# Two layer norms' neighbours reordered: when late weights are split, and in which order a product's three terms run

## The chip, the core and the metric

The kernel runs on one core of a Trainium2 chip. The core has a matrix engine (TensorE, PE in the profile, with its weight loads as PEld), a vector engine (VectorE, DVE), a scalar engine (ScalarE, ACT), GpSimd (POOL) and SyncE (SP), which here issues nearly all of the DMAs. Each engine works through its own queue in the order of the program, and waits on semaphores for the others. The metric is the device time of one execution in microseconds (us); lower is better.

## The reference, cut to what matters

One step of a two-layer decoder on 512 prompt rows and 8 sample rows, 1024 wide. Layer 0 mixes tokens with windowed attention, layer 1 with gated linear attention (GLA). A gated feed-forward net (FFN, 2816 wide) follows each, and a layer norm follows each mixer and each net.

```python
def layer_norm(x, g, b):
    mu = jnp.mean(xf, -1, keepdims=True)
    var = jnp.mean(jnp.square(xf - mu), -1, keepdims=True)
    return (xf - mu) * lax.rsqrt(var + LN_EPS) * g + b
...
def conv_ffn(x, buf, w_up, conv_w, conv_b, w_down):
    h = x @ w_up
    a, u = h[..., :D_FF], h[..., D_FF:]
    ap = jnp.concatenate([buf, a], axis=1)
    c = conv_b + sum(conv_w[j] * ap[:, j:j + T] for j in range(CONV_W))
    return (jax.nn.gelu(c, approximate=False) * u) @ w_down, ap[:, T:]
...
    for i in range(DEPTH):
        mix = swa(x) if i % 2 == 0 else gla_mix(x)
        x = layer_norm(ALPHA * x + mix, ln_mix_g[i], ln_mix_b[i])
        x = layer_norm(ALPHA * x + conv_ffn(x), ln_ffn_g[i], ln_ffn_b[i])
```

All of it is in float32, and the products keep nearly that precision. The kernel splits each operand into a high part in a shorter format (fp32r) and a low part, the rest, and sums three products: high by high, weight's high by rows' low, weight's low by rows' high.

## The kernel before, in words

**Tiles.** Activations lie transposed, 128 features by rows. The rows are in two groups: a (256 prompt rows; tiles `x_a`, `xs_a`) and b (256 prompt rows and the 8 sample rows; `x_b`, `xh_b`, `xl_b`). For group a high and low parts share the tile `xs_a`.

**Units.** The weights are cut into 187 units of 128 output columns. A unit is loaded by SP into one of two `raw` tiles (L160). ACT writes its high part `wh` and DVE its low part `wl = raw - wh`. The two lines for this are L165 and L168, or, for "late" units, L177 and L179 in `parts`. Units 0 to 9 are attention's, 10 to 17 its output product, 18 to 85 the first net, 86 (the small rank weight) to 110 GLA, 111 to 118 its output product, 119 to 186 the second net. Six `wts` slots hold units. At the start of each net one more unit (24 and 125) goes into an extra slot.

**Loop.** `order` (L970 onwards) interleaves the groups: group a runs ahead of group b by four or five units. At the start of the first net the steps are a18 to a23, b18, a24, b19, a25 and so on, where a18 is group a's product with unit 18. After each step of group b a further unit is loaded.

**Product.** `product` makes 24 matmuls of a unit, for eight slices of 128 features: L193 (high by high), L195 (rows' low), L196 (weight's low). For group a and the first unit of a net the rows' low parts come after all others, at L198. From the fifth pair of a net on, group a uses `product2` (L214, L215).

**Norm.** `ln_chunk` adds the output product and sums up; `ln_end` ends the norm. PE means the sums (L283), ACT takes mean and square (L291, L292), DVE the negated variance `nv` (L295), ACT logarithm and exponential (L304, L305), DVE refines the root (L311, L312) into `rp` (L314). Then for each of eight slices DVE scales (`x_b`, L333), ACT writes the high part (`xh_b`, L334) and DVE the low part (`xl_b`, L335). The first product of group b in the next phase needs `xh_b`. POOL subtracts the mean from six of the slices (L294).

**The net's steps.** For a gate unit ACT copies PE's result (L616) and starts the convolution (L621), DVE adds two taps (L622, L623), ACT takes GELU (L632, whose function table must be loaded first). For the value unit that follows, DVE multiplies (L644), and ACT and DVE split the result (L221, L222).

**What sets the order.** Within a stretch of code a scheduler places each engine's instructions by its own estimate of when operands are ready. `issue_after(ins)` makes what is written inside it stand behind `ins` in the same engine's queue. `parts` uses this for the five units loaded around a norm (19 to 23, 87 to 91, 120 to 124). While `norm` holds, for `HOLD` steps after group a's norm, the high parts go behind group a's exponential. The low part of the first goes behind group a's last `x_a`, the others behind its last low row. `norm[4]` is the number of the first of these units.

Of the kernel before, what the change touches and what calls it, by code (L numbers as in the profile page):

```python
# [14 lines left out]
AF = mybir.ActivationFunctionType  # L15
# [5 lines left out]
P = 128  # L21
D = 1024
KD = 8
# [31 lines left out]

LATEB = 14

HOLD = 5

WIDE = 4  # L60

# [16 lines left out]
def parted(rows):  # L78

    return rows.rearrange("p (j t) -> p t j", t=2)  # L80


def in_turn(rows):

    return rows.rearrange("p t j -> p j t")
# [10 lines left out]
class Net:  # L96
# [74 lines left out]
    def parts(self, u, h, l, r):  # L171


        norm = self.norm if self.norm and self.slot < self.norm[0] else None
        behind = lambda ins: self.tc.issue_after(ins) if norm else ExitStack()
        with behind(norm and norm[1]):
            self.nc.scalar.activation(h, r, AF.Copy)  # L177
        with behind(norm and norm[2 if u == norm[4] else 3]):
            self.nc.vector.tensor_tensor(l, r, h.bitcast(F32), op=ALU.subtract)  # L179
        yield from ()  # L180

    def product(self, g, u, rh, rl):
        nc = self.nc
        h, l = self.w[u]
        nt = self.units[u][1]

        tail = g.i == 0 and u in self.phases[2::3]
        ps = self.acc.tile([P, 512], F32, name="accp")
        o = ps[:, :g.n].rearrange("p (j t) -> p j t", t=2)
        for k in range(nt):  # L190
            ks = slice(k * P, (k + 1) * P)
            xh, xl = in_turn(rh[:, k]), in_turn(rl[:, k])
            nc.tensor.matmul(o, h[:, ks], xh, start=k == 0, stop=False)  # L193
            if not tail:
                nc.tensor.matmul(o, h[:, ks], xl, start=False, stop=False)  # L195
            nc.tensor.matmul(o, l[:, ks], xh, start=False, stop=not tail and k == nt - 1)  # L196
        for k in range(nt) if tail else ():
            nc.tensor.matmul(o, h[:, k * P:(k + 1) * P], in_turn(rl[:, k]), start=False, stop=k == nt - 1)  # L198
        return ps[:, :g.n]

    def product2(self, g, u, rs, rh, rl, wide):
# [76 lines left out]
    def ln_end(self, g, i, last=False):  # L278
        nc, n, x = self.nc, g.n, g.x
        yield 0 if g.i and not last else 1  # L280
        e1, e2 = self.mtile("tp")[:, :n], self.mtile("pv")[:, :n]
        for e, sums, rest in ((e1, g.s1, x[:, KD - 1]), (e2, g.s2, g.q)) if last else ((e1, g.s1, None), (e2, g.s2, None)):
            nc.tensor.matmul(e, self.ones_a, sums, start=True, stop=rest is None)  # L283
            if rest is not None:
                nc.tensor.matmul(e, self.ones_a, rest, start=False, stop=True)
        t = lambda name, b=1: self.ln.tile([P, NT - 256], F32, name=name, bufs=b)[:, :n]
        mu, q, nv, r = t("mu"), t("msq"), t("nv"), t("r")
        if last:

            nv, vr = self.mtile("sc")[:, :n], self.mtile("sc")[:, :n]  # L290
        nc.scalar.copy(mu, e1)  # L291
        nc.scalar.activation(q, e1, AF.Square)  # L292
        for m in range(2, NSUB) if last else range(NSUB):
            nc.gpsimd.tensor_tensor(x[:, m], x[:, m], mu, op=ALU.subtract)  # L294
        nvi = nc.vector.scalar_tensor_tensor(nv, q, LN_EPS, e2, op0=ALU.subtract, op1=ALU.subtract)  # L295

        with self.tc.issue_after(nvi.ins):
            if last:
                for xp in (x[:, 0:2], x[:, NSUB:KD]):
                    nc.vector.tensor_tensor(xp, xp, e1.unsqueeze(1).broadcast_to([P, 2, n]), op=ALU.subtract)  # L300
            else:
                for m in range(NSUB, KD):
                    nc.vector.tensor_tensor(x[:, m], x[:, m], e1, op=ALU.subtract)
        nc.scalar.activation(r, nv, AF.Ln, scale=-1.0)  # L304
        self.exp = nc.scalar.activation(r, r, AF.Exp, scale=-0.5).ins  # L305
        if last:
            nc.vector.tensor_tensor(vr, nv, r, op=ALU.mult)
            q = nv
            nc.vector.scalar_tensor_tensor(q, vr, 0.5, r, op0=ALU.mult, op1=ALU.mult)
        else:  # L310
            nc.vector.tensor_tensor(q, r, r, op=ALU.mult)  # L311
            nc.vector.scalar_tensor_tensor(q, q, 0.5, nv, op0=ALU.mult, op1=ALU.mult)  # L312
        rp = e2
        nc.vector.scalar_tensor_tensor(rp, q, 1.5, r, op0=ALU.add, op1=ALU.mult)  # L314
        sc = lambda m: self.par[:, C_LNG + i * KD + m:C_LNG + i * KD + m + 1]
        bi = lambda m: self.par[:, C_LNB + i * KD + m:C_LNB + i * KD + m + 1]
        if last:

            behind = None
            for m in range(0, KD, 2):  # L320
                xp = x[:, m:m + 2]
                with self.tc.issue_after(behind) if behind else ExitStack():
                    nc.vector.tensor_tensor(xp, xp, rp.unsqueeze(1).broadcast_to([P, 2, n]), op=ALU.mult)
                for j in (m, m + 1):
                    if j in (0, 1, 2, 4, 6):
                        nc.scalar.activation(x[:, j], x[:, j], AF.Identity, scale=sc(j), bias=bi(j))
                    else:
                        behind = nc.vector.tensor_scalar(x[:, j], x[:, j], sc(j), bi(j), op0=ALU.mult, op1=ALU.add).ins
                nc.sync.dma_start(out=self.O["y"][:, m:m + 2, g.c0:g.c0 + n], in_=xp)
            return  # L330

        for m in range(KD):
            v = nc.vector.scalar_tensor_tensor(x[:, m], x[:, m], sc(m), rp, op0=ALU.mult, op1=ALU.mult)  # L333
            nc.scalar.activation(g.xh[:, m], parted(x[:, m]), AF.Identity, bias=bi(m))  # L334
            xl = nc.vector.scalar_tensor_tensor(g.xl[:, m], parted(x[:, m]), bi(m), g.xh[:, m].bitcast(F32), op0=ALU.add, op1=ALU.subtract)  # L335
        if g.i == 0:
            self.norm = self.slot + HOLD, self.exp, v.ins, xl.ins, self.next_phase() + 1
        for m in range(KD):
            yield 1 if m else LATEB
            self.tc.keep_in_program_order(nc.gpsimd.tensor_scalar(x[:, m], x[:, m], 1.0, bi(m), op0=ALU.mult, op1=ALU.add))  # L340
# [655 lines left out]
    def next_unit(self, extra):  # L996
        u = self.nu
        if u < len(self.units):
            self.nu += 1
            done = u - WSLOTS  # L1000
            late = not extra and self.units[u][1] and any(e - 5 <= done < e for e in (*self.phases[2:3], *self.phases[3:4], *self.phases[5:6]))
            self.load_unit(u, extra=extra, late=late)
            if extra:
                self.extra[u] = True
# [147 lines left out]
```

## Time and profile before

| | |
|---|---|
| median of 3 runs | 1142.89 us (1142.06 to 1144.12) |
| the profiled execution's own time | 1142.6 us |
| its span, first to last instruction | 1140.9 us |
| mean granted TensorE clock | 0.990 of full |
| DVE, ACT, POOL busy | 68%, 50%, 28% of the span |

The span is what the profile's times are counted in, from 0. The profiled execution took 1.7 us more than its span, and lies 0.3 us under the median. Three norms stand between phases: the one before the first net (about 155 to 195 us), the one before GLA (515 to 558) and the one before the second net (755 to 795). A fourth ends the program and isn't touched.

### The profile page before, as it was taken

How to read it: one execution, taken by the hardware profiler on the slowest of the kernel's cores; microseconds unless marked ns; L12 is line 12 of the kernel's file. 1: busy time of each engine (PE TensorE's matmuls, PEld its weight loads, DVE VectorE, ACT ScalarE, POOL GpSimd, SP SyncE). 2: the span in 40 equal slices, each digit the busy share in tenths (PEclk: the TensorE clock that was granted, in tenths of full speed). 3: DMA queues.
4: the chain of work that ended last, by engine and by line, in shares of the span. 5: the costliest groups of instructions: out<-in, count | busy, mean ns of one | idle time of the engine just before them, and what ended most of it. 6: DMA issues, size and time to landing. Idle time of an engine off the chain costs nothing.

```text
span 1140.9 us, 22909 instructions
## 1 busy us (share of the span) xinstructions
PE 1103.6 (97%) x8806; PEld 1055.0 (92%) x8806; DVE 779.6 (68%) x1630; ACT 566.6 (50%) x1251; POOL 316.0 (28%) x585
## 2 busy tenths in 40 slices
PE   8998998999999999999899999998999999999996
PEld 7997798999999999999899899898999999999995
DVE  8897578755665566668867777788755665466566
ACT  5677556524553245435545555456534553245433
POOL 4575584400110011354311101274400110001242
PEclk9999999999999999999899999999999999999998
DMA  7463022333233233243124355432323323223222
GB/s 244 147 182 90 15 75 94 111 95 129 93 100 105 92 104 101 75 133 96 54 88 151 114 183 161 129 109 93 112 93 117 105 93 104 100 93 112 75 64 75
DMA packets 53788, 122.81 MB, mean 108 GB/s; under 512 B 6792, under 2 KB 27312, under 8 KB 53680
## 3 DMA queue, kind: packets, MB, share of 16 engines
q1 hardware_dynamic: 51664, 119.61, 32.5%
q10 hardware_dynamic: 2016, 1.75, 0.5%
q8 instruction: 69, 1.13, 0.4%
q14 instruction: 39, 0.32, 0.1%
HBM read 108.67 MB, written 8.47 MB: 103 GB/s over the span
## 4 chain that ended last, share of the span: by engine, by line
PE 75%; DVE 11%; DMA 6%; ACT 4%; issue 2%; POOL 1%; SPq 1%; ACTq 0%; DVEq 0%; POOLq 0%
PE accp L195 15%; PE accp L214 15%; PE accp L196 15%; PE accp L193 15%; PE accp L215 8%; DMA vb<-dv 3%; DVE wl L168 1%; DVE xs_a L335 1%; DMA qs<-hl 1%; DVE wl L179 1%; DVE sgla L889 1%; DMA raw<-in_w_qkv 1%; DMA raw<-in_w_up 1%; DVE x_a L333 1%; PE pv L533 1%
## 5 line engine op out<-in xcount | busy, mean ns | idle before, releaser
L168 DVE TENSOR_TENSOR wl<-raw,wh 128x1024 fp32r<-128x1024 f32 (+2 forms) x174 | 210.4, 1211 | 109.2 <-ACT wh L165 108.5
L165 ACT ACTIVATE wh<-raw 128x1024 fp32r<-128x1024 f32 (+2 forms) x170 | 175.8, 1034 | 208.9 <-PE accp L195 187.0
L193 PE MATMUL accp<-xh_b,wh 128*128 128x264 f32 x976 | 271.7, 278 | 6.5 <-ACT xh_b L334 6.5
L195 PE MATMUL accp<-xl_b,wh 128*128 128x264 f32 x976 | 270.7, 278 | 0.2 <-DVE xl_b L335 0.2
L196 PE MATMUL accp<-xh_b,wl 128*128 128x264 f32 x976 | 270.5, 277 | 0.0
L214 PE MATMUL accp<-xs_a,wh 128*128 128x512 f32 x576 | 196.3, 382 | 0.0
L193 PEld LDWEIGHTS accp<-xh_b,wh 128*128 128x128 f32 x976 | 184.9, 189 | 7.4 <-ACT xh_b L334 6.8
L195 PEld LDWEIGHTS accp<-xl_b,wh 128*128 128x128 f32 x976 | 184.5, 189 | 2.9 <-DVE xl_b L335 0.4
L196 PEld LDWEIGHTS accp<-xh_b,wl 128*128 128x128 f32 x976 | 184.4, 189 | 0.8 <-issue 0.6
L215 PE MATMUL accp<-xs_a,wl 128*128 128x256 f32 x576 | 145.4, 273 | 0.0
L193 PE MATMUL accp<-hh_b,wh 128*128 128x264 f32 x480 | 133.9, 279 | 1.8 <-ACT hh_b L221 1.3
L195 PE MATMUL accp<-hl_b,wh 128*128 128x264 f32 x480 | 134.4, 280 | 0.3 <-DVE hl_b L573 0.2
L196 PE MATMUL accp<-hh_b,wl 128*128 128x264 f32 x480 | 133.5, 278 | 0.0
L214 PEld LDWEIGHTS accp<-xs_a,wh 128*128 128x128 f32 x576 | 109.1, 189 | 11.4
L193 PE MATMUL accp<-xs_a,wh 128*128 128x256 f32 x400 | 112.9, 284 | 2.1 <-ACT wh L165 0.9
L196 PE MATMUL accp<-xs_a,wl 128*128 128x256 f32 x400 | 111.6, 281 | 1.6 <-DVE wl L168 1.1
L215 PEld LDWEIGHTS accp<-xs_a,wl 128*128 128x128 f32 x576 | 110.2, 191 | 1.9
L195 PE MATMUL accp<-xs_a,wh 128*128 128x256 f32 x384 | 107.9, 281 | 0.0
L193 PEld LDWEIGHTS accp<-hh_b,wh 128*128 128x128 f32 x480 | 91.3, 190 | 2.5 <-ACT hh_b L221 1.7
L195 PEld LDWEIGHTS accp<-hl_b,wh 128*128 128x128 f32 x480 | 91.2, 190 | 1.8 <-DVE hl_b L573 0.4
L196 PEld LDWEIGHTS accp<-hh_b,wl 128*128 128x128 f32 x480 | 91.3, 190 | 0.2
L225 POOL COPY hist<-aext 128x2 f32<-128x2 f32 x44 | 10.8, 245 | 276.8 <-DVE aext L620 274.0
(331 smaller groups left out, 2488.8 us busy)
## 6 DMA issues: line engine op xcount, KB each, us to landing
raw<-in_w_up SPq DMA_DIRECT2D x88, 512.0 KB, 3.4
raw<-in_w_down SPq DMA_DIRECT2D x32, 512.0 KB, 3.4
raw<-in_w_gla SPq DMA_DIRECT2D x24, 512.0 KB, 3.4
raw<-in_w_mix_o SPq DMA_DIRECT2D x16, 512.0 KB, 4.0
raw<-in_w_down SPq DMA_DIRECT2D x16, 384.0 KB, 3.1
qs<-hl SPq DMA_DIRECT2D x64, 64.0 KB, 2.1
sgla<-in_state_gla SPq DMA_DIRECT2D x16, 256.0 KB, 2.8
vb<-dv SPq DMA_DIRECT2D x16, 256.0 KB, 3.8
```

What stands on the lines that cost most here:

```text
L165: nc.scalar.activation(h[:, c], r[:, c], AF.Copy)
L168: nc.vector.tensor_tensor(l[:, c], r[:, c], h[:, c].bitcast(F32), op=ALU.subtract)
L179: self.nc.vector.tensor_tensor(l, r, h.bitcast(F32), op=ALU.subtract)
L193: nc.tensor.matmul(o, h[:, ks], xh, start=k == 0, stop=False)
L195: nc.tensor.matmul(o, h[:, ks], xl, start=False, stop=False)
L196: nc.tensor.matmul(o, l[:, ks], xh, start=False, stop=not tail and k == nt - 1)
L214: both = lambda: nc.tensor.matmul(o, h[:, ks], in_turn(rs[:, k].rearrange("p t q j -> p t (q j)")), start=k == 0, stop=last)
L215: low = lambda: nc.tensor.matmul(o[:, :P], l[:, ks], in_turn(rh[:, k]), start=False, stop=False)
L333: v = nc.vector.scalar_tensor_tensor(x[:, m], x[:, m], sc(m), rp, op0=ALU.mult, op1=ALU.mult)
L335: xl = nc.vector.scalar_tensor_tensor(g.xl[:, m], parted(x[:, m]), bi(m), g.xh[:, m].bitcast(F32), op0=ALU.add, op1=ALU.subtract)
L533: mm = nc.tensor.matmul(pv[64 * v:64 * v + 64, b * P:(b + 1) * P], self.vtok[:, kb, 64 * v:64 * v + 64], parts[v][w][:, b], start=i == 0, ...
L889: late(nc.vector.scalar_tensor_tensor(s[:, j], vb[:, j], kraw[:, b:b + 1], s[:, j], op0=ALU.mult, op1=ALU.add))
```

## The change

```diff
-HOLD = 5
+HOLD = 6
+
+LOWS = 7
...
         norm = self.norm if self.norm and self.slot < self.norm[0] else None
         behind = lambda ins: self.tc.issue_after(ins) if norm else ExitStack()
-        with behind(norm and norm[1]):
+
+        n = u - norm[4] if norm else 0
+        with behind(norm and (*[norm[1]] * 4, self.square, self.exp)[n]):
             self.nc.scalar.activation(h, r, AF.Copy)
-        with behind(norm and norm[2 if u == norm[4] else 3]):
+        with behind(norm and (norm[2], *[norm[3]] * 4, self.rest)[n]):
             self.nc.vector.tensor_tensor(l, r, h.bitcast(F32), op=ALU.subtract)
...
-        tail = g.i == 0 and u in self.phases[2::3]
+        tail = u in self.phases[2::3] or g.i and u in self.phases[2:4]
+        behind = g.i == 0 and nt == KD and not tail and any(e < u < e + LOWS for e in (*self.phases[2:4], *self.phases[5:6]))
...
-            nc.tensor.matmul(o, l[:, ks], xh, start=False, stop=not tail and k == nt - 1)
-        for k in range(nt) if tail else ():
-            nc.tensor.matmul(o, h[:, k * P:(k + 1) * P], in_turn(rl[:, k]), start=False, stop=k == nt - 1)
+            if not behind:
+                nc.tensor.matmul(o, l[:, ks], xh, start=False, stop=not tail and k == nt - 1)
+        for k in range(nt) if tail or behind else ():
+            w, r = (h, rl) if tail else (l, rh)
+            nc.tensor.matmul(o, w[:, k * P:(k + 1) * P], in_turn(r[:, k]), start=False, stop=k == nt - 1)
...
-        nc.scalar.activation(q, e1, AF.Square)
+        self.square = nc.scalar.activation(q, e1, AF.Square).ins
...
+        self.rest = xl.ins
         if g.i == 0:
             self.norm = self.slot + HOLD, self.exp, v.ins, xl.ins, self.next_phase() + 1
...
-            late = not extra and self.units[u][1] and any(e - 5 <= done < e for e in (*self.phases[2:3], *self.phases[3:4], *self.phases[5:6]))
+            late = self.units[u][1] and any(e - 5 <= done < e + extra for e in (*self.phases[2:3], *self.phases[3:4], *self.phases[5:6]))
```

The parts of the late weights are tied to group b's norm as well. For the fifth (units 23, 91, 124) the high part goes behind group b's square (L292 before, L299 now). The extra unit (24, 125) becomes a sixth late one: its high part goes behind group b's exponential, its low part behind group b's last low row. GLA has no extra unit, so no sixth.

In `product`, group a's matmuls with the weight's low part come after the unit's other sixteen, for units 19 to 24, 87 to 92 and 120 to 125. Group b now takes its rows' low parts last in units 18 and 119, as group a did. No instruction is added or taken away on PE, DVE, ACT or POOL, and SP's queue keeps its order.

The change's lines have other numbers. What was L165, L168, L177, L179 is now L167, L170, L181, L183. The matmuls L193, L195, L196, L198 are L198, L200, L202, L205. From the norm on seven lines are added, from the net's steps on eight.

On ACT, in group b's norm before the first net, these rows stand one after the other before the change. `wh_2624`, `wh_2660`, `wh_2737` are the high parts of units 22, 23 and 24; `mu`, `msq`, `r` belong to the norm:

```order
L177 ACTIVATE wh_2624<-raw_2623 128x1024
L177 ACTIVATE wh_2660<-raw_2659 128x1024
L291 COPY mu_2674<-tp_2670 128x264
L292 ACTIVATE msq_2675<-tp_2670 128x264
L616 COPY aext_2832<-accp_2807 128x256
L621 ACTIVATE conv_2835<-accp_2807,par_78 128x256
L304 ACTIVATE r_2677<-nv_2676 128x264
L305 ACTIVATE r_2677<-r_2677 128x264
L632 ACT_TABLE_LOAD
L632 ACTIVATE conv_2770<-conv_2770 128x256
L165 ACTIVATE wh_2737<-raw_2736 128x1024
L632 ACTIVATE conv_2835<-conv_2835 128x256
```

And after it:

```order
L181 ACTIVATE wh_2624<-raw_2623 128x1024
L298 COPY mu_2674<-tp_2670 128x264
L299 ACTIVATE msq_2675<-tp_2670 128x264
L181 ACTIVATE wh_2660<-raw_2659 128x1024
L311 ACTIVATE r_2677<-nv_2676 128x264
L624 COPY aext_2832<-accp_2807 128x256
L629 ACTIVATE conv_2835<-accp_2807,par_78 128x256
L312 ACTIVATE r_2677<-r_2677 128x264
L640 ACT_TABLE_LOAD
L640 ACTIVATE conv_2768<-conv_2768 128x256
L181 ACTIVATE wh_2737<-raw_2736 128x1024
L228 ACTIVATE hs_a_87<-hprod_2803 128x2x128
```

The mean and the square moved ahead of unit 23's high part, and the two steps of the net that stood ahead of the logarithm now stand behind it.

On DVE, in the same norm, from `nv` to the scaled rows, before:

```order
L295 SCALAR_TENSOR_TENSOR nv<-msq,pv 128x264
L303 TENSOR_TENSOR x_b<-x_b,tp 128x264 x2
L622 SCALAR_TENSOR_TENSOR conv<-aext,par,conv 128x256
L311 TENSOR_TENSOR msq<-r 128x264
L623 SCALAR_TENSOR_TENSOR conv<-aext,par,conv 128x256
L644 TENSOR_TENSOR hprod<-conv,accp 128x256
L312 SCALAR_TENSOR_TENSOR msq<-msq,nv 128x264
L168 TENSOR_TENSOR wl<-raw,wh 128x1024
L644 TENSOR_TENSOR hprod<-conv,accp 128x256
L314 SCALAR_TENSOR_TENSOR pv<-msq,r 128x264
L222 TENSOR_TENSOR hs_a<-hprod,hs_a 128x2x128
L333 SCALAR_TENSOR_TENSOR x_b<-x_b,par,pv 128x264 x8
```

And after:

```order
L302 SCALAR_TENSOR_TENSOR nv<-msq,pv 128x264
L310 TENSOR_TENSOR x_b<-x_b,tp 128x264 x2
L183 TENSOR_TENSOR wl<-raw,wh 128x1024
L630 SCALAR_TENSOR_TENSOR conv<-aext,par,conv 128x256
L318 TENSOR_TENSOR msq<-r 128x264
L652 TENSOR_TENSOR hprod<-conv,accp 128x256
L631 SCALAR_TENSOR_TENSOR conv<-aext,par,conv 128x256
L319 SCALAR_TENSOR_TENSOR msq<-msq,nv 128x264
L229 TENSOR_TENSOR hs_a<-hprod,hs_a 128x2x128
L321 SCALAR_TENSOR_TENSOR pv<-msq,r 128x264
L652 TENSOR_TENSOR hprod<-conv,accp 128x256
L340 SCALAR_TENSOR_TENSOR x_b<-x_b,par,pv 128x264 x8
```

Unit 23's low part, which stood ahead of `nv`, comes after it. Unit 24's low part (L168) left this stretch; it stands behind the last `xl_b`.

On PE, where group b's first product (`accp_2933`) meets unit 24 of group a (`accp_2975`; `accp_2904` is unit 23), before:

```order
L195 MATMUL accp_2904<-xs_a_86,wh_2660 128x256
L196 MATMUL accp_2904<-xs_a_86,wl_2661 128x256
L193 MATMUL accp_2933<-xh_b_89,wh_2404 128x264
L193 MATMUL accp_2975<-xs_a_86,wh_2737 128x256
L195 MATMUL accp_2975<-xs_a_86,wh_2737 128x256
L196 MATMUL accp_2975<-xs_a_86,wl_2738 128x256
```

And after:

```order
L205 MATMUL accp_2904<-xs_a_86,wl_2661 128x256 x8
L198 MATMUL accp_2933<-xh_b_89,wh_2404 128x264
L202 MATMUL accp_2933<-xh_b_89,wl_2405 128x264
...
L198 MATMUL accp_2975<-xs_a_86,wh_2737 128x256
L200 MATMUL accp_2975<-xs_a_86,wh_2737 128x256
```

Before, one matmul of b18 was followed by all 24 of a24. Now two slices of b18 come first, and the other six alternate with a24's first sixteen. The first `xh_b` matmul has the same number of matmuls ahead of it as before, in all three phases.

## The prediction

> **What bounds the kernel now.** I read the page's busy shares first, then PE's list of waits, then the order of time around the three norms.
>
> ```profile
> span 1140.9 us, 22909 instructions
> PE 1103.6 (97%) x8806; PEld 1055.0 (92%) x8806; DVE 779.6 (68%) x1630; ACT 566.6 (50%) x1251; POOL 316.0 (28%) x585
> PE accp L193 <- ACT xh_b L334: 6.5, 2, 3.3
> PE accp L716 <- ACT v_a L783: 2.5, 1, 2.5
> ```
>
> PE is busy for 97% of the span. The change adds no matmul and takes none away, so it can only win idle time, 37 us in all, or clock. The list of waits (total, times, longest) says where: two waits for `xh_b`, 6.5 us together, and one of 2.5 us at GLA's start, where ACT's `v_a` copy stands behind the first `xh_b`. PE's own rows at these places, with the idle time before each in brackets:
>
> ```profile
> 188.48 0.38 PE L193 MATMUL accp<-xh_b,wh 128*128 128x264 f32 x1 [3.27 <-ACT xh_b L334]
> 191.87 0.38 PE L195 MATMUL accp<-xl_b,wh 128*128 128x264 f32 x1 [0.22 <-DVE xl_b L335]
> 787.44 0.59 PE L193 MATMUL accp<-xh_b,wh 128*128 128x264 f32 x1 [3.19 <-ACT xh_b L334]
> 784.00:787.40 3.40, 0.26 (x3) 0.07 (x1) 3.40 (x7) 1.66 (x6) 1.83 (x4) 0.99 0.28 57
> 787.40:790.60 3.20, 3.16 (x14) 3.05 (x15) 3.20 (x9) 2.98 (x7) 0.00 (x0) 0.50 0.27 109
> 556.95 0.39 PE L193 MATMUL accp<-xs_a,wh 128*128 128x256 f32 x1
> 547.50:555.90 8.40, 8.25 (x31) 6.99 (x32) 6.66 (x18) 4.26 (x11) 0.00 (x0) 0.59 0.00 0
> ```
>
> The rows with a colon are stretches of time: length, then busy time of PE, PEld, DVE, ACT and POOL, then the granted clock. After the wait at the second net the clock is 0.50 for 3.2 us. After the wait at GLA's start it is 0.59 on the mean for 8.4 us. After the equally long wait at the first net it stays at 1.00 (page and stretches show no fall there).
>
> So the question is what holds `xh_b`. ACT and DVE, first net:
>
> ```profile
> 175.62 1.06 ACT L177 ACTIVATE wh<-raw 128x1024 fp32r<-128x1024 f32 x1 [1.90 <-DMA raw<-in_w_up]
> 178.13 1.06 ACT L177 ACTIVATE wh<-raw 128x1024 fp32r<-128x1024 f32 x1 [1.45 <-DMA raw<-in_w_up]
> 179.09 0.36 ACT L291 COPY mu<-tp 128x264 f32<-128x264 f32 x1
> 180.82 0.42 ACT L304 ACTIVATE r<-nv 128x264 f32<-128x264 f32 x1 [0.34 <-DVE nv L295]
> 181.27 0.42 ACT L305 ACTIVATE r<-r 128x264 f32<-128x264 f32 x1
> 181.71 1.28 ACT L632 ACT_TABLE_LOAD   x1
> 183.01 0.42 ACT L632 ACTIVATE conv<-conv 128x256 f32<-128x256 f32 x1
> 183.33 1.06 ACT L165 ACTIVATE wh<-raw 128x1024 fp32r<-128x1024 f32 x1
> 184.59 0.46 ACT L221 ACTIVATE hs_a<-hprod 128x256 fp32r<-128x256 f32 x1
> 187.89 2.40 ACT L334 ACTIVATE xh_b<-x_b,par 128x264 fp32r<-128x264 f32 x5
> 184.69 1.76 DVE L168 TENSOR_TENSOR wl<-raw,wh 128x1024 fp32r<-128x1024 f32 x1
> 186.37 0.41 DVE L644 TENSOR_TENSOR hprod<-conv,accp 128x256 f32<-128x256 f32 x1
> 186.70 0.43 DVE L314 SCALAR_TENSOR_TENSOR pv<-msq,r 128x264 f32<-128x264 f32 x1
> 187.05 0.41 DVE L222 TENSOR_TENSOR hs_a<-hprod,hs_a 128x256 fp32r<-128x256 f32 x1
> 187.38 3.28 DVE L333 SCALAR_TENSOR_TENSOR x_b<-x_b,par,pv 128x264 f32<-128x264 f32 x8
> ```
>
> The mean waits behind unit 23's high part (178.13), which waits for its DMA. Further on, unit 24's low part (184.69, 1.76 us) stands in DVE's queue between the norm's steps. Neither belongs to the norm.
>
> **The change, part by part (first net).** The mean moves ahead of unit 23's high part: from 179.09 to 176.58, when unit 22's ends. That alone frees little, because unit 23's high part now stands ahead of the logarithm: 178.13 + 0.96 (the step from its start to the next, 179.09 - 178.13) = 179.09, where the logarithm was at 180.82. Then L616 (estimate 0.32 later), L621 (0.25), and after 0.46 the exponential at 180.12 instead of 181.27: 1.15 us won.
>
> From there I use the rows' steps. Table load at 180.56, GELU at 181.86 (+1.30), ending at 182.28. DVE's `hprod` 182.30; ACT's unit 24 high part 182.18, then `hs_a` at 183.14, done 183.60. DVE works off L623 and L312 until about 183.85, then L222, L314 and the second `hprod`, 0.33 to 0.35 each, and reaches `x_b` at about **184.87 instead of 187.38**. The other part won, 1.36 us, is unit 24's low part (1.76) less what DVE now waits for `hs_a`. `xh_b` of the first slice follows after about 1.05, and PE starts at 185.92 instead of 188.48.
>
> That isn't the whole account, since the rest arrives slice by slice. ACT's eight `xh_b` step by 0.48, and L616 and L621 (0.85) now stand after the second: the third slice is there at 187.6, the last at about 189.8. Against that PE has 16 matmuls of b18 and 16 of a24, alternating:
>
> ```profile
> 783.87 0.28 PE L195 MATMUL accp<-xs_a,wh 128*128 128x256 f32 x1
> 783.98 0.28 PE L196 MATMUL accp<-xs_a,wl 128*128 128x256 f32 x1
> ```
>
> A matmul starts each 0.11 us, so the 32 take 3.6 us. Without waits PE would end them at 185.2 + 3.6 = 188.8; starting the third slice at 187.65 with 24 matmuls or so to go it ends them at about 190.4. Idle time left: **1.6 us**. Before it was 3.27 + 0.22 = 3.49. Term one: **-1.9**. Its bounds are -0.2 (only the exponential's 1.15 is won, less the 0.9 that the slices cost) and -2.6 (the slices cost nothing).
>
> The second net has the same rows 1.03 us apart in phase (3.19 idle, 1.6 left). Term two: **-1.6**, bounds 0 and -2.5.
>
> **Clock.** In the stretch 787.40 to 790.60 half the clock costs half of 3.2 us. With no gap over 0.8 us I take the fall as gone: term three **-1.6**; the other end is 0. The Trainium skill (TensorE: Matmul & The Clock Gate, What's actually happening) says that the clock halves after a whole idle window of about 3.4 us. By that rule a gap of 3.19 us is no cause, the fall would stay, and the sum would lose this term.
>
> **GLA's start.**
>
> ```profile
> 538.03 1.06 ACT L177 ACTIVATE wh<-raw 128x1024 fp32r<-128x1024 f32 x1 [1.31 <-DMA raw<-in_w_gla]
> 540.91 0.41 ACT L304 ACTIVATE r<-nv 128x264 f32<-128x264 f32 x1
> 546.18 3.29 DVE L333 SCALAR_TENSOR_TENSOR x_b<-x_b,par,pv 128x264 f32<-128x264 f32 x8
> 552.54 0.89 DVE L335 SCALAR_TENSOR_TENSOR xl_b<-x_b,par,xh_b 128x264 fp32r<-128x264 f32 x2
> 555.56 0.38 ACT L718 COPY z_b<-accp 128x264 f32<-128x264 f32 x1 [0.27 <-PE accp L716]
> 555.83 1.06 ACT L165 ACTIVATE wh<-raw 128x1024 fp32r<-128x1024 f32 x1
> ```
>
> Here unit 91 holds the mean (538.03). Its move brings the logarithm from 540.91 to 539.5, DVE's `x_b` by the same steps to about 544.7, the last low row (553.43) to 552.0. PE's rank product then ends near 552.1, `z_b` and unit 92's high part follow, and dense work resumes at about 554.9 instead of 556.95. But in the new order PE has work left over then that it had done before (three transposes, L811 twice and L822: about 1.1 us at full clock). Term four: **-0.8**. PE will be thinly fed for seven microseconds, so the low clock may last: one more stretch like 787.40 to 790.60 costs 1.6, the end +0.8; with no fall at all it is -2.5.
>
> **What I cost at nothing.** Three terms of a unit in another order are the same 24 matmuls. Short waits of PE ahead of the first `xh_b` may come or go, but that moment is set by ACT and DVE. Unit 24's low part lands at about 192.1 to 193.3, behind the last `xl_b`; its eight matmuls are due at about 193.5. It holds a `raw` tile, so SP's load of unit 26 is later:
>
> ```profile
> 186.48 0.33 SPq L160 DMA_DIRECT2D raw<-in_w_up  x1
> DMA to landing us min/median/max: 3.2/3.4/4.8
> 200.00 1.22 DVE L168 TENSOR_TENSOR wl<-raw,wh 128x1024 fp32r<-128x1024 f32 x1
> 205.23 0.38 PE L214 MATMUL accp<-xs_a,wh 128*128 128x512 f32 x1
> ```
>
> Issued at 193.4 instead of 186.48, it lands by 198.2, and both parts are there by about 200.9. PE wants them at 205.23 less 1.9. Beyond these 2.4 us each microsecond would cost one.
>
> **Rivals.**
> *The clock falls all the same* (chance 0.25). For it: the fall at GLA's start, and this one, where PE was far from idle for a whole stretch:
>
> ```profile
> 133.00:134.00 1.00, 0.46 (x3) 0.30 (x3) 0.96 (x3) 0.43 (x2) 1.00 (x3) 1.00 0.00 0
> ...
> 135.00:136.00 1.00, 1.00 (x9) 1.00 (x8) 0.00 (x0) 0.09 (x1) 0.92 (x3) 0.71 0.00 0
> ```
>
> It gives 1138.6, or 1140.2 if GLA's fall also lasts one stretch longer. The skill's rule above gives 1138.6 too.
> *The norm isn't earlier* (0.15): between exponential and `x_b` there now stand, on two engines by turns, table load, GELU, unit 24's high part and two splits. If these take what the old way took, 1.15 is won and 0.9 given back in each net, nothing at GLA, and the clock falls: 1142.4.
> *Slower* (0.05): unit 24's high part waits for its DMA, issued at 177.97 when unit 22's low part (176.71 + 1.22) frees the tile, and the whole norm now waits behind it. A landing after 6.1 us eats the 1.9; after 8.0 us `xh_b` comes 1.2 later than before and with the slices each net loses 2.1: 1142.9 + 4.2 - 0.8 = 1146.3. Against it: 4.8 is the longest landing in the rows.
>
> **How the numbers follow.** Forecast (0.55): 1142.6 - 1.9 - 1.6 - 1.6 - 0.8 = 1136.7 for the profiled execution, which lay 0.3 under the median: **1137.0**. The low end takes both nets at -2.6 and -2.5 and GLA at -1.9: 1134.3. The high end, 1141.0, takes in the first rival and some of the second. A measurement of this kernel can tell about 0.2%, 2.3 us, from no change. Faster than that (under 1140.6): 0.76, the forecast and nearly all of the first rival. Within: 0.18. Slower: 0.06.
>
> **What would show it.** Right: PE's wait ahead of the first `xh_b` under 1 us in both nets, then several of under 0.5; a clock of 1.00 there; logarithm directly after a weight's high part; `x_b` starting 2.5 us earlier relative to PE's last group a matmul. Wrong: a wait on unit 24's DMA in ACT's rows, DVE idle for `hs_a` for over a microsecond, a half clock longer than 8 us after GLA's start, or PE waiting for unit 26.

## The result, and the profile after

The changed kernel takes **1135.95 us** (median of 6 runs, 1134.89 to 1137.74), against 1142.4 us before (6 runs): a ratio of 0.995, with a 95% interval of 0.9935 to 0.9964. The forecast was 1137.0 us, range 1134.3 to 1141.0. The profiled execution took 1136.07 us, its span is 1134.3 us.

First the page's busy shares of the changed kernel, then PE's list of waits (total, times, longest):

```profile
PE 1102.8 (97%) x8806; PEld 1053.7 (93%) x8806; DVE 781.7 (69%) x1630; ACT 565.7 (50%) x1251; POOL 317.3 (28%) x585
```

```profile
PE accp L724 <- ACT v_a L791: 2.0, 1, 2.0
PE accp L198 <- ACT xh_b L341: 1.9, 2, 1.0
```

The same matmuls, and the two waits for `xh_b` are down from 6.5 to 1.9 us. To see where the rest went, the program is cut into stages at an event that all versions have: PE's first matmul for the sums of group a's norm, four times. Before (L283) and after (L290):

```profile
156.07 0.59 PE L283 MATMUL tp<-s_a,ones_a 128*128 128x256 f32 x2
515.71 0.59 PE L283 MATMUL tp<-s_a,ones_a 128*128 128x256 f32 x2
754.35 0.48 PE L283 MATMUL tp<-s_a,ones_a 128*128 128x256 f32 x1
1115.29 0.38 PE L283 MATMUL tp<-s_a,ones_a 128*128 128x256 f32 x1
```

```profile
156.68 0.59 PE L290 MATMUL tp<-s_a,ones_a 128*128 128x256 f32 x2
514.16 0.59 PE L290 MATMUL tp<-s_a,ones_a 128*128 128x256 f32 x2
751.11 0.70 PE L290 MATMUL tp<-s_a,ones_a 128*128 128x256 f32 x2
1108.87 0.59 PE L290 MATMUL tp<-s_a,ones_a 128*128 128x256 f32 x2
```

The stage from the first row to the second holds group b's norm and the first net, the next holds GLA's start and GLA, the last the second net. Their lengths changed by **-2.16, -1.69 and -3.18 us**. Attention, which the change doesn't touch, was 0.61 longer in this execution; what follows 1108.87 was 0.2 shorter.

In the first net, rows of ACT, DVE and PE of the changed kernel (its times lie 0.6 later up to there):

```profile
177.16 0.36 ACT L298 COPY mu<-tp 128x264 f32<-128x264 f32 x1
178.96 1.07 ACT L181 ACTIVATE wh<-raw 128x1024 fp32r<-128x1024 f32 x1 [1.14 <-DMA raw<-in_w_up]
179.94 0.40 ACT L311 ACTIVATE r<-nv 128x264 f32<-128x264 f32 x1
180.96 0.41 ACT L312 ACTIVATE r<-r 128x264 f32<-128x264 f32 x1
183.01 1.06 ACT L181 ACTIVATE wh<-raw 128x1024 fp32r<-128x1024 f32 x1
185.62 3.28 DVE L340 SCALAR_TENSOR_TENSOR x_b<-x_b,par,pv 128x264 f32<-128x264 f32 x8
192.83 1.22 DVE L183 TENSOR_TENSOR wl<-raw,wh 128x1024 fp32r<-128x1024 f32 x1
184.79 1.06 PE L205 MATMUL accp<-xs_a,wl 128*128 128x256 f32 x8
186.72 0.38 PE L198 MATMUL accp<-xh_b,wh 128*128 128x264 f32 x1 [0.88 <-ACT xh_b L341]
782.05 0.38 PE L198 MATMUL accp<-xh_b,wh 128*128 128x264 f32 x1 [1.03 <-ACT xh_b L341]
```

The reader sees the forecast chain: the logarithm directly behind unit 23's high part, `x_b` 2.4 us earlier once the 0.6 is taken off (187.38 before), PE waiting 0.88 in place of 3.27 (in the second net, last row, 1.03 in place of 3.19), and unit 24's low part (192.83) behind the norm. What PE had to do behind that wait had another order, which turned out to matter as much as the earlier norm.

### The profile page after: what moved, and what is told of

It is laid out like the page before. It is cut to its first block, busy times and chain, and to the rows that moved or that the text cites. A ratio compares the mean times of both kernels' runs of the same rounds, so it can differ in the third digit from the quotient of the medians.

```text
span 1134.3 us, 22914 instructions
## 1 busy us (share of the span) xinstructions
PE 1102.8 (97%) x8806; PEld 1053.7 (93%) x8806; DVE 781.7 (69%) x1630; ACT 565.7 (50%) x1251; POOL 317.3 (28%) x585
## 4 chain that ended last, share of the span: by engine, by line
PE 75%; DVE 12%; DMA 6%; ACT 3%; issue 2%; POOL 1%; SPq 1%; ACTq 0%; DVEq 0%; POOLq 0%
PE accp L198 16%; PE accp L221 15%; PE accp L200 15%; PE accp L202 15%; PE accp L222 8%; DMA vb<-dv 3%; DVE wl L183 1%; DVE xs_a L342 1%; DMA qs<-hl 1%; DVE wl L170 1%; DVE sgla L897 1%; DMA raw<-in_w_up 1%; DMA raw<-in_w_qkv 1%; DVE x_a L340 1%; PE pv L541 1%
## 5 line engine op out<-in xcount | busy, mean ns | idle before, releaser
L170 DVE TENSOR_TENSOR wl<-raw,wh 128x1024 fp32r<-128x1024 f32 (+2 forms) x172 | 207.5, 1208 | 104.0 <-ACT wh L167 102.5
L198 PE MATMUL accp<-xh_b,wh 128*128 128x264 f32 x976 | 272.5, 279 | 1.9 <-ACT xh_b L341 1.9
L167 ACT ACTIVATE wh<-raw 128x1024 fp32r<-128x1024 f32 (+2 forms) x168 | 173.7, 1034 | 201.8 <-PE accp L200 186.5
L202 PE MATMUL accp<-xh_b,wl 128*128 128x264 f32 x976 | 270.8, 277 | 0.0
L200 PE MATMUL accp<-xl_b,wh 128*128 128x264 f32 x960 | 266.5, 278 | 0.0
L198 PEld LDWEIGHTS accp<-xh_b,wh 128*128 128x128 f32 x976 | 184.8, 189 | 3.5 <-ACT xh_b L341 2.5
L202 PEld LDWEIGHTS accp<-xh_b,wl 128*128 128x128 f32 x976 | 184.5, 189 | 0.8 <-issue 0.6
L200 PEld LDWEIGHTS accp<-xl_b,wh 128*128 128x128 f32 x960 | 181.6, 189 | 2.5 <-issue 0.4
L222 PE MATMUL accp<-xs_a,wl 128*128 128x256 f32 x576 | 145.4, 273 | 0.0
L198 PE MATMUL accp<-hh_b,wh 128*128 128x264 f32 x480 | 133.4, 278 | 1.7 <-ACT hh_b L228 1.2
L200 PE MATMUL accp<-hl_b,wh 128*128 128x264 f32 x480 | 133.7, 279 | 0.3 <-DVE hl_b L581 0.2
L202 PE MATMUL accp<-hh_b,wl 128*128 128x264 f32 x480 | 132.9, 277 | 0.0
L221 PEld LDWEIGHTS accp<-xs_a,wh 128*128 128x128 f32 x576 | 109.1, 189 | 11.4
L198 PE MATMUL accp<-xs_a,wh 128*128 128x256 f32 x400 | 107.6, 284 | 2.2 <-ACT xs_a L228 1.3
L200 PE MATMUL accp<-xs_a,wh 128*128 128x256 f32 x384 | 102.8, 281 | 0.0
L198 PEld LDWEIGHTS accp<-hh_b,wh 128*128 128x128 f32 x480 | 90.9, 189 | 2.4 <-ACT hh_b L228 1.6
L200 PEld LDWEIGHTS accp<-hl_b,wh 128*128 128x128 f32 x480 | 90.8, 189 | 1.8 <-DVE hl_b L581 0.4
L202 PEld LDWEIGHTS accp<-hh_b,wl 128*128 128x128 f32 x480 | 90.7, 189 | 0.2
L198 PEld LDWEIGHTS accp<-xs_a,wh 128*128 128x128 f32 x400 | 77.3, 194 | 3.4 <-issue 1.8
```

Of the source, the lines that this page charges most:

```text
L167: nc.scalar.activation(h[:, c], r[:, c], AF.Copy)
L170: nc.vector.tensor_tensor(l[:, c], r[:, c], h[:, c].bitcast(F32), op=ALU.subtract)
L221: both = lambda: nc.tensor.matmul(o, h[:, ks], in_turn(rs[:, k].rearrange("p t q j -> p t (q j)")), start=k == 0, stop=last)
L222: low = lambda: nc.tensor.matmul(o[:, :P], l[:, ks], in_turn(rh[:, k]), start=False, stop=False)
```

## The experiments

Ratios are to the kernel before, on the same chip; the medians come from several chips, so kernels are compared by their ratios. Stages are differences to the one profile of the kernel before, by the rows above. The last column counts the half-clock stretches of 3.4 us at the first net, at GLA's start and at the second net, found by stretches of 0.1 us.

| kernel | median, us | ratio (95%) | first net, GLA, second net, us | stretches |
|---|---|---|---|---|
| before | 1142.4 | | | 0, 2, 1 |
| the change | 1135.95 | 0.995 (0.9935-0.9964) | -2.16, -1.69, -3.18 | 0, 3, 0 |
| after_again | 1137.02 | 0.995 (0.9926-0.9974) | -2.29, -2.08, -3.20 | 0, 3, 0 |
| e1_parts_only | 1144.55 | 1.0009 (0.9993-1.0024) | +1.35, -0.96, -1.32 | 1, 2, 0 |
| e2_order_only | 1142.77 | 0.9992 (0.9977-1.0006) | +0.94, -1.15, +1.43 | 1, 1, 2 |
| e3_fifth_only | 1139.63 | 0.9971 (0.9957-0.9985) | -1.67, +0.80, -0.76 | 0, 3, 1 |
| e4_sixth_only | 1138.32 | 0.9952 (0.9933-0.9971) | -1.05, -2.16, -0.92 | 0, 1, 1 |
| e5_rows_low_in_place | 1136.94 | 0.9951 (0.9935-0.9967) | -1.79, -1.54, -2.52 | 0, 2, 0 |
| e6_weights_low_in_place | 1138.61 | 0.9972 (0.9955-0.9989) | -1.09, -0.26, -2.14 | 0, 2, 0 |
| v5_pool4 | 1135.21 | 0.9933 (0.9916-0.995) | -2.95, -0.60, -3.47 | 0, 3, 0 |
| v5_again | 1136.17 | 0.993 (0.9908-0.9952) | -2.77, +0.94, -3.69 | 0, 3, 0 |
| v6_pool2 | 1134.75 | 0.9921 (0.9902-0.994) | -3.05, -1.52, -3.93 | 0, 3, 0 |
| v6_pool4_root | 1134.93 | 0.9926 (0.9908-0.9945) | -3.06, +0.11, -4.03 | 0, 3, 0 |
| v7_nets_only | 1134.32 | 0.9925 (0.9907-0.9943) | -2.64, -1.96, -3.90 | 0, 0, 0 |

The changed kernel and its repeat agree within 0.13 us in both nets, v5_pool4 and its repeat within 0.22, and v6_pool2 and v7_nets_only, which have the same code for the nets, within 0.41. GLA differs by 0.4 in the change and its repeat, and by 1.5 in the two runs of v5: a wait for `sg` near 628 us was 0.8 in the change, 2.1 in e3 and 2.6 in v5_again, whose edits don't touch it. So nets are compared by stages, differences under some 0.4 us are not resolved there, and GLA is read with caution.

### Splits alone, order alone

e1 keeps the moved splits and gives the products their old order:

```diff
-        tail = u in self.phases[2::3] or g.i and u in self.phases[2:4]
+        tail = g.i == 0 and u in self.phases[2::3]
-        behind = g.i == 0 and nt == KD and not tail and any(...)
+        behind = g.i == 0 and nt == KD and not tail and False
```

> The weights' parts move as in the change; the products keep their old order. Theory A (the moved splits make the gain, the order of a product's terms is worth nothing, as the prediction had it): x_b starts some 2.4 us earlier in both nets and the time is 1136 to 1137.5 us. Rival B (splits and order only work together): unit 24's low part now comes behind group b's last low row, so PE can't use group a's product with unit 24 to fill the gaps between the slices of xh_b and xl_b; PE then waits slice by slice, some 3 us in each net, what the earlier x_b won is given back, and the time is 1142 to 1146 us.

e2 does the opposite:

```diff
-        with behind(norm and (*[norm[1]] * 4, self.square, self.exp)[n]):
+        with behind(norm and norm[1]):
...
-        with behind(norm and (norm[2], *[norm[3]] * 4, self.rest)[n]):
+        with behind(norm and norm[2 if u == norm[4] else 3]):
...
-            late = self.units[u][1] and any(e - 5 <= done < e + extra for e in ...)
+            late = self.units[u][1] and not extra and any(e - 5 <= done < e for e in ...)
```

and sets `HOLD` back to 5.

> The products have the change's order; the weights' parts are split as before. Theory A: ACT and DVE reach xh_b no earlier, both waits of PE stay at about 3.2 us, and so does the half clock at the second net; the time is 1141.5 to 1143 us. Rival C (the order alone makes most of it, by letting PE run on between the slices): 1137 to 1139.5 us. At GLA both see a wait of 0.5 us for a weight's low part go away.

Measured: 1.0009 and 0.9992. **Neither half has a gain by itself that the whole time shows**; theory A falls in e1, rival B holds, and in e2 theory A holds. By stages e1 isn't neutral: it loses 1.35 us in the first net, where the clock falls, and wins 1.32 in the second, where the fall of the kernel before is gone. PE's waits in e1 over the whole span, and its rows in the first net:

```profile
PE accp L200 <- DVE xl_b L342: 2.9, 2, 1.4
PE accp L198 <- ACT xh_b L341: 1.9, 2, 1.0
```

```profile
186.28 0.38 PE L198 MATMUL accp<-xh_b,wh 128*128 128x264 f32 x1 [0.92 <-ACT xh_b L341]
186.49 0.27 PE L198 MATMUL accp<-xs_a,wh 128*128 128x256 f32 x1
186.60 0.28 PE L200 MATMUL accp<-xs_a,wh 128*128 128x256 f32 x1
187.43 0.38 PE L198 MATMUL accp<-xh_b,wh 128*128 128x264 f32 x1 [0.55 <-ACT conv L629]
189.25 0.47 PE L200 MATMUL accp<-xl_b,wh 128*128 128x264 f32 x1 [1.44 <-DVE xl_b L342]
```

The first `xh_b` is as early as in the change. But after two matmuls of unit 24 the third needs that unit's low part, which now comes last of all on DVE, so the scheduler puts the rest of group a's product behind group b's: PE waits 0.55 and 1.44 us more (rival B expected some 3), and the clock falls for one stretch. In e2 the long wait stays, in both nets:

```profile
PE accp L198 <- ACT xh_b L341: 6.7, 2, 3.7
```

So the late split frees DVE and ACT ahead of `xh_b`, and the product order keeps PE fed although that low part is late.

### Which order

e5 takes group b's order back, e6 group a's; each is one of the two edits of e1.

> Of the change's product orders only group a's (weight's low parts last) is kept; group b's units 18 and 119 take the rows' low part slice by slice again. PE then has all of group a's unit 24 ahead of the second slice, but ends group b's first unit only at the pace of the low rows. If group a's order is what lets the late split pay: 1136 to 1138 us, waits for xl_b under 1 us. If group b's order carries it: waits for xl_b of 1 to 2 us in each net and 1139 to 1142 us.

> Of the change's product orders only group b's (rows' low parts last in units 18 and 119) is kept; group a takes the weight's low part in place again. Group a's unit 24 needs a low part that comes behind the last low row, so it can't fill the gaps between group b's slices. If group b's order suffices: 1136 to 1138 us. If group a's order carries it: PE waits slice by slice in both nets, 2 to 3 us each, and the time is 1139 to 1143 us.

Measured: 0.9951 and 0.9972. Against e1 (+1.35, -1.32), group a's order alone (e5) makes the nets 3.1 and 1.2 us shorter, group b's alone (e6) 2.4 and 0.8, both 3.5 and 1.9. In the first net some 1.7 of it is the fall of the clock, which e1 has there and these don't. Either gives PE something to do between the slices. Group a's is nearly enough; the waits for `xl_b` in e5 are 1.1 us over both nets, as against 2.9. e6's time lies between its two expected ranges: PE's rows show one wait of 0.9 in the first net, and no wait for `xl_b`, where matmuls with `xh_b` of group b's own first units now stand between the slices.

### Which split

e3 leaves units 24 and 125 where the scheduler puts them (`late = self.units[u][1] and not extra and ...`); e4 leaves the fifth's high part behind group a's exponential (`(*[norm[1]] * 5, self.exp)[n]`).

> The change without the sixth late unit: units 24 and 125 are split where the scheduler puts them. Theory A with the prediction's terms: the exponential comes 0.9 us earlier in each net, but the low part of unit 24 (1.76 us) again stands ahead of the root's last step, so about 1 us of the 2.4 is won in each net and all of GLA's 1.7: 1138 to 1140 us. If the fifth alone carries it: 1136 to 1137. If it carries nothing in the nets: about 1141.

> The change with the fifth late unit's high part where it was, behind group a's exponential, ahead of the mean. Theory A: x_b comes about 1.4 us earlier in each net (the low part of unit 24 gone from DVE's queue), the exponential stays where it was, GLA wins only the 0.5 us of a weight's low part: 1138 to 1140 us. If the sixth alone carries it: 1136 to 1137.

Measured: 1139.63 and 1138.32 us, within both expected ranges. PE's waits of e3, then of e4:

```profile
PE accp L198 <- ACT xh_b L341: 4.4, 2, 2.3
```

```profile
PE accp L198 <- ACT xh_b L341: 4.2, 2, 2.1
```

Each moves `xh_b` about half of the way, and a wait of 2.1 to 2.3 us is still enough for a fall of the clock at the second net. In the nets the fifth wins 1.67 and 0.76 us, the sixth 1.05 and 0.92; their sums, 2.72 and 1.68, lie a little above the change's 2.16 and 1.47 (3.18 less one stretch of 1.71). The expected terms for GLA missed both times: e3 should have won 1.7 there and lost 0.8, e4 should have won 0.5 and won 2.16. e4's whole time can't be told from the change's (intervals overlap), although its profile wins 3.4 us less in the nets and 0.5 at most more at GLA; the profiled execution, 1140.09 us, was the slowest of its six.

### The clock, again

> The changed kernel once more, beside the others of this call. Expected: 0.994 to 0.996 of before. In the trace the half clock should again come in stretches of a multiple of 3.4 us; where they lie should follow from how much PE did in the 3.4 us ahead, not from one gap's length alone: none at the nets, two or three of them at GLA's start.

The ratio came out at 0.995 and the stretches as expected. In every profile the granted clock changes only at points a multiple of 3.41 us apart. In the kernel before it falls at 135.4, 548.4 and 787.3: the distances are 121 and 70 times 3.413. Stretches cut at these points, in the kernel before (length, then busy time of PE, PEld, DVE, ACT, POOL, the granted clock, DMA):

```profile
183.22:186.63 3.41, 1.99 (x18) 1.79 (x17) 3.41 (x5) 1.83 (x4) 3.35 (x5) 1.00 0.01 2
186.63:190.04 3.41, 1.56 (x14) 1.56 (x15) 3.41 (x10) 3.22 (x8) 0.29 (x2) 1.00 0.39 154
190.04:193.45 3.41, 3.19 (x29) 3.00 (x28) 3.41 (x10) 1.68 (x4) 0.00 (x0) 1.00 0.00 0
783.97:787.38 3.41, 0.29 (x3) 0.10 (x1) 3.41 (x7) 1.67 (x6) 1.86 (x4) 1.00 0.26 49
787.38:790.79 3.41, 3.35 (x15) 3.24 (x16) 3.41 (x10) 3.00 (x8) 0.00 (x0) 0.50 0.27 109
```

This answers why the prediction found a fall behind one wait of 3.2 us and none behind the other. At the first net the wait lay across a boundary, and each stretch had 14 to 18 matmuls. At the second it lay within one stretch, which had 3, and the next one got half the clock. e2 has the same two waits, in another place against the grid, and the clock falls at both nets:

```profile
184.83:188.24 3.41, 0.76 (x6) 0.76 (x7) 3.41 (x9) 2.42 (x7) 1.04 (x3) 1.00 0.44 153
188.24:191.65 3.41, 3.41 (x18) 3.41 (x17) 3.41 (x10) 2.23 (x6) 0.00 (x0) 0.50 0.00 1
782.16:785.57 3.41, 1.14 (x11) 0.95 (x9) 3.41 (x7) 1.63 (x4) 3.00 (x4) 1.00 0.01 2
785.57:792.40 6.83, 5.44 (x25) 5.44 (x26) 6.83 (x19) 4.32 (x11) 0.18 (x1) 0.50 0.26 79
```

At the nets, in all the profiles, stretches at full clock with up to 11 matmuls (PE busy for 1.3 us or less) were followed by half the clock, and those with 13 and more weren't. That is no rule for the whole program: at GLA's start the clock fell behind stretches in which PE was busy for up to 2.83 us (13 matmuls, v6_pool4_root), and in attention, at 135.4 in the kernel before, behind one with 2.69 us and 21 matmuls. What exactly is counted stays open. From attention to the second net a stretch at half clock was followed by another where it held 7 to 11 matmuls, and by the full clock where it held 13 to 21. The Trainium skill (TensorE: Matmul & The Clock Gate, What's actually happening) has the window, 3413 ns and free-running, and the trace agrees. It asks for an idle window, and here PE was at work for 1.14 us of 3.41 and the clock still fell. So a fall costs up to 1.71 us a stretch (half of 3.41), and whether a gap of 2.1 to 3.7 us causes one is partly a matter of where it lies. At the nets a single gap of 1.3 us or less, as the change leaves them (0.88 and 1.03), didn't cause one in any profile.

### What is late next: POOL beside DVE

In the change's norm DVE is busy nearly all the time from the variance to `x_b`, and some of its steps take twice their time. The same step in the change, and in v5_pool4, where POOL takes four slices of the mean in place of six:

```profile
182.45 0.97 DVE L318 TENSOR_TENSOR msq<-r 128x264 f32<-128x264 f32 x1
```

```profile
181.97 0.42 DVE L319 TENSOR_TENSOR msq<-r 128x264 f32<-128x264 f32 x1
```

```diff
-        for m in range(2, NSUB) if last else range(NSUB):
+        nsub = 4 if g.i and not last else NSUB
+        for m in range(2, NSUB) if last else range(nsub):
...
-                for m in range(NSUB, KD):
+                for m in range(nsub, KD):
```

> The change, and group b's norm subtracts the mean from four slices on POOL and four on DVE in place of six and two (the last norm as it was). In the profile of the change DVE's steps of the norm take 0.97 us beside POOL's subtractions and 0.42 us after them; DVE gets 0.76 us more work and POOL's 6.4 us end about 2.1 us sooner. If DVE's slow steps come from POOL's work beside them: x_b starts about 1 us sooner in both nets and the time is about 1 to 3 us under the change's. If they don't: x_b starts 0.8 us later and the time is 1 to 2 us over it.

> The change with four slices of group b's mean on POOL, once more. Expected: 0.992 to 0.995 of before; steps of 0.42 us on DVE once POOL's four subtractions are over.

> The change with two slices of group b's mean on POOL and six on DVE (1.5 us more work on DVE than in the change, POOL's subtractions over after 2.2 us). If the cover by POOL costs DVE more than the slices themselves: x_b starts earlier again and the time is 1 us under that with four. If four was about the best: x_b starts 0.5 us or more later, and the time is equal or up to 2 us over it.

Measured: 0.9933 and 0.993 with four slices on POOL, 0.9921 with two. POOL's four subtractions end at about 181.7 and DVE's step at 181.97 takes 0.42; in the change POOL's six run until 184.0. Counted from group a's sums, `x_b` of the first net starts at 28.94 in the change (28.80 in its repeat), at 28.16 and 28.34 with four and at 28.19 with two: 0.5 to 0.8 us sooner where about 1 was expected, and no sooner with two than with four. So neither of v6_pool2's two readings holds whole: the ratio is 1 us lower than with four, within the intervals, but `x_b` isn't earlier. The nets' stages get 0.3 to 0.8 us shorter with four than in the change, and 0.7 to 0.9 with two (0.5 and 0.7 in v7_nets_only, with the same code there); PE hardly waits any more in the first net:

```profile
185.54 0.38 PE L198 MATMUL accp<-xh_b,wh 128*128 128x264 f32 x1 [0.18 <-ACT xh_b L342]
```

The Trainium skill (GPSIMD Engine Reference, 1. Specifications) says that GpSimd shares its SBUF interfaces with VectorE, with contention for instructions with two SBUF inputs; the step above has two. In the change a step that reads one operand from PSUM, the memory that PE writes its sums (`accp`) to, isn't slowed beside POOL's subtractions:

```profile
183.35 0.41 DVE L652 TENSOR_TENSOR hprod<-conv,accp 128x256 f32<-128x256 f32 x1
```

The whole times overlap with the change's by their intervals, so the gain of v6_pool2 over the change, 1.2 to 1.6 us, is shown in the nets' stages only.

v6_pool4_root, with four slices on POOL, also moves the fifth's high part behind group b's exponential, and its low part behind the root's last step (`self.root`, the instruction that writes `rp`).

> Four slices on POOL, and of the fifth unit (23, 91, 124) the high part goes behind group b's exponential in place of its square, the low part behind the root's last step. The logarithm then waits for the variance alone, about 0.5 to 1 us sooner. Theory D (DVE, fully busy from the variance to x_b, now sets x_b, and PE needs the fifth's low part before x_b): no gain, or a wait of PE for that low part, 1135 to 1138 us. Theory E (ACT's chain still sets x_b): x_b 1 us sooner and 1132.5 to 1134.5 us.

0.9926: `x_b` starts 0.3 us sooner than with four slices alone (182.47 against 184.40, but attention was 1.6 shorter), PE doesn't wait for `xh_b` at the first net, and the nets win 0.1 to 0.3 and 0.3 to 0.6 over the two runs of v5. The whole time, 1134.93 us, lies between the two expected ranges and shows no gain, which is nearer to theory D; the wait of PE for the low part, which it named as possible, didn't come (PE has one wait of 0.20 for a late high part, in the second net).

### GLA's start

In the change the half clock lasts three stretches there, 10.24 us (here with the stretch ahead of them), as against two before:

```profile
541.12:544.53 3.41, 1.44 (x13) 1.25 (x12) 3.41 (x10) 1.44 (x5) 0.32 (x1) 1.00 0.20 82
544.53:554.80 10.27, 10.16 (x34) 8.28 (x35) 7.84 (x21) 5.91 (x14) 0.00 (x0) 0.50 0.05 9
```

and PE's first matmul of dense work there:

```profile
552.84 0.56 PE L198 MATMUL accp<-xs_a,wh 128*128 128x256 f32 x1
```

To see what the start alone wins, DVE's scan of group a's third head is a mark ahead of the wait for `sg`. In the change, then in e2, where the fifth isn't moved:

```profile
601.35 0.68 DVE L742 TENSOR_TENSOR_SCAN dcum<-reset,dmn 128x256 f32<-128x256 f32 x1
```

```profile
602.33 0.68 DVE L742 TENSOR_TENSOR_SCAN dcum<-reset,dmn 128x256 f32<-128x256 f32 x1
```

Counted from group a's sums (514.16, and 515.87 in e2) that is 87.19 us in the change, 86.46 in e2, 87.75 before (603.46 - 515.71). The repeat of the change has 87.50, the other kernels with the fifth moved have 87.1 to 87.6 (88.2 in v6_pool4_root), and e4, where it isn't moved either, 86.29. So the start wins 0.56 and 0.25 in the change's two profiles and **1.29 and 1.46 without the fifth moved**. Of the change's and of e2's gain, 0.4 is won ahead of group b's sums, where PE waited for a weight's low part in the kernel before:

```profile
PE accp L196 <- DVE wl L179: 0.5, 1, 0.5
```

e1 and e6, which have group a's old order there, lack it. What is left is 0.2 or nothing with the fifth moved and 0.9 without. That the earlier norm is paid back at half clock fits the count of stretches, one in e2 and e4 against two or three, but it isn't shown: e5 and e6, with two stretches, reach the mark no sooner (87.24 and 87.21) than the change with three.

v7_nets_only is v6_pool2 with the fifth's high part moved in the nets alone:

```diff
-        with behind(norm and (*[norm[1]] * 4, self.square, self.exp)[n]):
+        with behind(norm and (*[norm[1]] * 4, norm[1] if self.phases[3] < u < self.phases[4] else self.square, self.exp)[n]):
```

> The change with two slices of group b's mean on POOL, and the fifth late unit's high part behind group b's square in the two nets only; at GLA (unit 91) it stays behind group a's exponential, as before the change. Theory F (at GLA the earlier norm wins nothing by 603 us, since the half clock lasts three stretches of 3.4 us instead of one or two): the half clock at GLA's start is one or two stretches, group a's third head is 0.5 to 0.9 us earlier against the norm's sums than with the fifth moved, and the time is 1133.5 to 1135 us. Theory G (the earlier norm is worth its 0.8 us there): three stretches or not, GLA is 0.5 to 1 us slower, 1135.5 to 1137 us.

Its profile has no half clock at GLA's start, and the third head's scan comes 84.83 us after the sums (597.08 - 512.25), 2.3 less than in v6_pool2. But it then waits 2.3 us for `sg`, GLA's whole stage is only 0.4 shorter, and the ratio, 0.9925, is v6_pool2's. Theory F has the direction right at the start (no stretch in place of its one or two, 2.3 us in place of 0.5 to 0.9), and theory G falls, since GLA isn't slower. But this is one profile, and how much of the 2.3 us is the edit and how much the place against the clock's grid is open; that a shorter start makes a shorter program isn't shown. v6_pool2, v6_pool4_root and v7_nets_only (0.9921 to 0.9926) can't be told apart.

## Why the prediction was right, point by point

- **The first net's chain** held step by step. With the 0.6 us of attention taken off: logarithm at 179.3 (forecast 179.09), exponential at 180.3 (180.12), `x_b` at 185.0 (184.87), first product at 186.1 (185.92). One reason in it didn't hold: `x_b` doesn't wait for `hs_a`. DVE has no idle time from 180.06 to `x_b`, and steps that POOL slows took the time instead. Term -1.9, measured -2.16. PE's rows show 0.9 us of idle time left where 1.6 was forecast; but behind fresh slices matmuls start 0.21 us apart in place of 0.11, which the rows count as busy, and PE's busy time in the stage grew by 0.43.
- **The second net's** term, -1.6, measured -1.47 (3.18 less a stretch of 1.71).
- **The clock there**, -1.6, measured -1.71. The reason given, no gap over 0.8 us, is close: the gap was 1.03, just past the 1 us that the prediction named as a sign of being right. The first rival, that the clock falls all the same, fell, and with it the reading that a gap of 3.19 is no cause; the missing piece was the grid.
- **GLA**, -0.8, measured -1.69 and -2.08 in two profiles. Dense work began 38.7 us after group a's sums (552.84 - 514.16) in place of 41.2 (556.95 - 515.71): 2.6 us earlier, forecast 2.1. The low clock lasted one stretch longer, as the term's upper bound had it; at 10.24 us it was longer than the 8 us that the prediction named as a sign of being wrong, and that sign came true. The term was mis-sized, and its sign is right partly by luck: the start won 0.56 and 0.25, of which 0.4 is the wait for a weight's low part that wasn't in the sum. The rest came later in GLA, where e3, with the change's GLA code, lost 0.8; it stays open whether it belongs to the change.
- **The sum** is closer than its terms. They add up to -5.9 and the three stages to -7.03; attention, 0.61 longer in this execution, took part of the difference back.
- **What was costed at nothing**: "Three terms of a unit in another order are the same 24 matmuls." This step failed. The account of the idle time did count on group a's 16 matmuls of unit 24 to alternate with group b's, but it took that as given. Without the order the splits win nothing that the whole time shows (1.0009). It didn't spoil the sum only because the change has both. In the same paragraph the load of unit 26 was right. SP's issues from 185 to 200 us, and their time to landing:

```profile
L162 SPq DMA_DIRECT2D raw<-in_w_up x3: 328/328/328, 194.1 to 199.9; - x3
DMA to landing us min/median/max: 3.4/3.4/3.4
```

The first was issued at 194.1 (forecast 193.4 and 0.6 of attention), and PE has no wait on a weight there.
- **The other rivals**: "the norm isn't earlier" fell with `x_b` 2.4 us earlier. The slower case needed a landing of over 6.1 us; unit 24's high part ran at 183.01 with no wait for its DMA (no idle time ahead of its row).

## What to carry to other kernels

A split that is moved out of a chain must not be the operand that the matrix engine's filler work needs: move the filler's own order along with it, and test the two apart, since here each half alone gave nothing that the whole time shows. Measure a stage between two events that no version moves: the nets repeated there within 0.02 to 0.4 us in kernels whose whole time varies by several us. And before explaining why one gap cost clock and an equal one didn't, cut the profile at the clock's own grid.

## What the runs showed of the hardware that was not expected

- The granted clock moves on a fixed grid of 3.41 us, not aligned with the program. At the nets half the clock followed stretches in which PE was busy for 0.3 to 1.3 us, not only idle ones; elsewhere it followed stretches with up to 2.87 us (attention, v5_again).
- A DVE step with both operands in SBUF takes 0.97 us beside POOL's subtractions and 0.42 us alone, and one with an operand in PSUM 0.41 beside them. With four of the mean's slices on POOL in place of six, DVE, with more work of its own, reached `x_b` 0.5 to 0.8 us sooner.
